# Splitting the weights of later phases during the Mamba phase, and storing the parts

## The chip, the cores and the metric

The kernel runs on one core of one Trainium2 chip. The metric is device time in microseconds (us) of one execution. A core has five instruction queues that run on their own: TensorE (PE, matmuls and transposes, results in PSUM), VectorE (DVE), ScalarE (ACT), GpSimd (POOL) and SyncE (SP, which here issues nearly all DMAs, that is, transfers between DRAM and the on-chip memory SBUF). Each queue is served strictly in order. An instruction that has to wait (for a semaphore that another engine or a landed DMA raises) holds up everything behind it on its own queue.

## What is computed

The reference is one layer of a hybrid encoder over 4096 tokens of width 1024. All three groups of heads read the same normalised input:

```python
h = rmsnorm(x, pre_norm_w)
u = h @ w_in                               # 1024 x 3208
y_ssm  = mamba2_group(u[:, :1544], ...)    # conv, chunked scan, gate, norm
y_rwkv = rwkv7_group(u[:, 1544:2696], ...) # r, k, v, g, decay latents; delta-rule state
y_mem  = memory_xattn_group(u[:, 2696:], mem_k, mem_v)
x + rmsnorm(concat(y_ssm, y_rwkv, y_mem) @ w_out, post_norm_w)
```

`mem_k` and `mem_v` are one projection, `rmsnorm(mem) @ w_mem_kv`, of 256 memory tokens. Everything is float32.

## The kernel before

**How a large product is done.** A float32 product is made from two rounded operands. Each matrix is split into a part in the type float32r, called hi, and the rounded remainder, called lo. The product is then three matmuls, hi*hi, hi*lo and lo*hi, for each of the 8 blocks of 128 rows. `proj_cm` (L145) and `proj_tm` (L155) issue them. For the input, `split_T` makes the two parts once for each stripe of 256 tokens, and `store_hT` writes them to DRAM (`hTd`), so that later phases read them back finished with `load_hT`.

**How the weights are split.** A raw weight block `w_st` is loaded by DMA (L70); ACT multiplies it with the norm's weight into hi (L80), and DVE forms lo in one instruction from the raw block, the same scale and hi (L81). For the output projection there is no scale (L85, L86). `split_w` and `load_w` do this at the place where a phase starts, so the weights of a phase are split at its seam with the phase before.

**The phases.** There are 16 stripes. `phase_a` (Mamba) loops over them: `stage1` of stripe i (z, x, B, C projections, convolution) is woven with `stage2` of stripe i-1 (the scan) and with `build_hT` of stripe i+1. `phase_b` (RWKV) starts with the last `stage2` as a tail beside its own first `stage1`, for which `load_b` loads and splits five matrices (the latents `lat`, then k, r, v, g). `stage1` first projects `lat`, then the first half of k, and then calls `lora`, whose matmuls (L642) need `wls`, made from the small tile `wl` (L556). Then it loops over the stripes. `phase_c` starts beside the tail of the RWKV recurrence: `memory` loads the memory tokens `mt` (L1076), normalises and transposes them (L132) and projects them with two split matrices; `qg` projects the queries with weights that `load_qg` split (L1015, L1016); `load_o` and `load_o2` split the two halves of the output weights `wo0` and `wo1`. Then it loops over the stripes.

**What sets the order.** `weave` takes the next piece of work from several generators in proportion to weights, and a scheduler places the instructions on each queue by a model of when each is ready. So a change in one place can move rows on every engine, but on the chip the rows of a queue are fixed. Buffers are tiles of pools with a fixed number of slots; a slot's next use waits for the last reader of its former one. `stage2` uses POOL for five large instructions for each chunk of 128 tokens, two chunks a stripe: `xde` (L427), `xst` (L428), `y` (L452), `prev` (L449) and a mask on `R` (L406). `R` is a row of decays, stored and read back by DMA (L382, L386). The convolution is 24 DVE instructions for each stripe (L338).

## Time and profile before

| | |
|---|---|
| time, median of 3 runs (lowest, highest) | 2209.92 us (2208.5, 2213.29) |
| the profiled execution's own time | 2211.41 us |
| its span, first to last instruction | 2209.6 us |
| busy: PE / DVE / ACT / POOL | 97% / 68% / 53% / 33% of the span |
| Mamba loop | to about 748 us, about 46 us for each stripe |
| seam of Mamba and RWKV | about 727 to 842 us |
| RWKV loop, seam to phase C | to about 1455 us, about 1455 to 1650 us |

A row of a timeline gives the start in us, the duration in us, the engine, the line and operation with output and inputs, how many equal rows were merged (x4), and in brackets the idle time of that engine before it and what ended it. A row of groups gives busy time in us and the mean of one in ns, and then idle time before it. A row of windows gives, for a stretch of time, the busy time of each engine and its number of instructions, then the granted TensorE clock as a share of full speed, the busy share of the DMA engines and GB/s. DMA-issuing rows of SP are marked SPq.

### The profile page before, as it was taken

Reading aid. Unit: us, or ns where it says so; the run is one execution under the profiler, and the core shown is the slowest. Engines: PE = TensorE matmul, PEld = TensorE weight load, DVE = VectorE, ACT = ScalarE, POOL = GpSimd, SP = SyncE. Lnnn points to the kernel's source line nnn. Section 1 sums busy time; section 2 is a strip of 40 time slices with the busy share of each in tenths; the row PEclk is TensorE's granted clock in tenths of the full one; section 3 lists DMA queues with packets and bytes.
Section 4 is the critical chain, followed back from the end, with each engine's and each line's share of the span. In section 5 each row is a group of like instructions: output and inputs, shape, how many; then the busy total and the mean of one; then the engine's idle time right before and its main releaser. Section 6 shows DMA issues by size and latency. Waiting matters only on the chain.

```text
span 2209.6 us, 50991 instructions
## 1 busy us (share of the span) xinstructions
PE 2151.8 (97%) x20705; PEld 1982.7 (90%) x20705; DVE 1502.7 (68%) x3405; ACT 1181.1 (53%) x2873; POOL 726.7 (33%) x1043
## 2 busy tenths in 40 slices
PE   8999999999999889999999999998999999999998
PEld 8999999999999788898898998987888888888986
DVE  7778788878888876577776777777573444444452
ACT  7555555555553565566666666677553333333441
POOL 2443443434433333334334333333112222222223
PEclk9999999999999999999999999999899999999999
DMA  6422233222332321111111121123243334333332
GB/s 212 148 97 87 97 134 106 97 87 96 131 109 106 118 87 40 45 64 63 50 45 45 45 83 49 45 89 129 83 172 134 125 110 162 110 133 132 100 123 77
DMA packets 82570, 218.86 MB, mean 99 GB/s; under 512 B 8151, under 2 KB 44446, under 8 KB 70046
## 3 DMA queue, kind: packets, MB, share of 16 engines
q1 hardware_dynamic: 81294, 215.59, 28.3%
q8 instruction: 163, 2.67, 0.5%
q14 instruction: 73, 0.60, 0.1%
q10 hardware_dynamic: 1040, 0.00, 0.0%
HBM read 152.00 MB, written 63.57 MB: 98 GB/s over the span
## 4 chain that ended last, share of the span: by engine, by line
PE 84%; DVE 7%; DMA 4%; ACT 3%; issue 1%; POOL 1%; SPq 0%; POOLq 0%; ACTq 0%; DVEq 0%
PE ps_pj L145 40%; PE ps_yd L155 8%; PE ps_pj L155 8%; PE ps_st L155 8%; DVE cc L338 2%; DMA R<-rowd 1%; PE ps_yd L467 1%; PE ps_yd L772 1%; PE ps_pj L1185 1%; PE ps_tr L132 1%; PE ps_yo L920 1%; PE ps_tr L1173 1%; PE ps_yo L927 1%; PE ps_st L459 1%; PE ps_yo L937 1%
## 5 line engine op out<-in xcount | busy, mean ns | idle before, releaser
L145 PE MATMUL ps_pj<-hh,w_hi 128*128 128x256 f32 x2704 | 790.5, 292 | 10.4 <-DVE cm L613 6.1
L145 PE MATMUL ps_pj<-hh,w_lo 128*128 128x256 f32 x2704 | 780.1, 289 | 0.2 <-DVE w_lo L81 0.2
L145 PE MATMUL ps_pj<-hl,w_hi 128*128 128x256 f32 x2704 | 777.2, 287 | 0.0
L145 PEld LDWEIGHTS ps_pj<-hh,w_hi 128*128 128x128 f32 x2704 | 520.2, 192 | 21.1 <-issue 6.3
L145 PEld LDWEIGHTS ps_pj<-hh,w_lo 128*128 128x128 f32 x2704 | 519.5, 192 | 6.8 <-DVE w_lo L81 0.7
L145 PEld LDWEIGHTS ps_pj<-hl,w_hi 128*128 128x128 f32 x2704 | 520.3, 192 | 5.9
L338 DVE SCALAR_TENSOR_TENSOR cc<-ux,cwh,cc 128x256 f32<-128x256 f32 x384 | 218.0, 610 | 15.4 <-ACT cc L335 15.1
L155 PE MATMUL ps_pj<-w_hi,hh 128*128 128x256 f32 (+1 forms) x528 | 155.6, 295 | 4.1 <-DVE zs L299 2.8
L155 PE MATMUL ps_pj<-w_lo,hh 128*128 128x256 f32 (+1 forms) x528 | 153.0, 290 | 0.0
L155 PE MATMUL ps_pj<-w_hi,hl 128*128 128x256 f32 (+1 forms) x528 | 152.2, 289 | 0.0
L1192 DVE TENSOR_TENSOR ya<-ps_pj,ya 64x256 f32<-64x256 f32 x64 | 26.9, 421 | 121.4 <-ACT ya L1191 121.0
L155 PEld LDWEIGHTS ps_pj<-w_hi,hh 128*128 128x128 f32 x528 | 102.1, 194 | 6.2 <-DVE zs L299 3.3
L1225 POOL TENSOR_TENSOR xr<-ot,xr 128x512 f32<-128x512 f32 x64 | 89.0, 1412 | 43.1 <-DVE ot L1224 43.1
L1219 POOL TENSOR_TENSOR sq<-sq 128x1 f32<-128x1 f32 x32 | 6.6, 207 | 292.9 <-ACT ot L1217 292.9
L155 PEld LDWEIGHTS ps_pj<-w_lo,hh 128*128 128x128 f32 x528 | 102.2, 194 | 0.3
L155 PEld LDWEIGHTS ps_pj<-w_hi,hl 128*128 128x128 f32 x528 | 102.0, 193 | 0.0
L155 PE MATMUL ps_st<-wo1l,yh 128*128 128x512 f32 x248 | 97.7, 394 | 1.0 <-DVE wo1l L1286 1.0
L155 PE MATMUL ps_yd<-wo0h,yh 128*128 128x512 f32 x248 | 98.2, 396 | 0.0
L155 PE MATMUL ps_st<-wo1h,yh 128*128 128x512 f32 x248 | 97.5, 393 | 0.0
L155 PE MATMUL ps_st<-wo1h,ylo 128*128 128x512 f32 x248 | 97.4, 393 | 0.0
L155 PE MATMUL ps_yd<-wo0h,ylo 128*128 128x512 f32 x248 | 97.3, 392 | 0.0
L155 PE MATMUL ps_yd<-wo0l,yh 128*128 128x512 f32 x248 | 97.2, 392 | 0.0
(468 smaller groups left out, 5106.8 us busy)
## 6 DMA issues: line engine op xcount, KB each, us to landing
hl<-hTd SPq DMA_DIRECT2D x32, 1024.0 KB, 5.1
hh<-hTd SPq DMA_DIRECT2D x32, 1024.0 KB, 8.3
xt<-in_x_dram SPq DMA_DIRECT2D x32, 512.0 KB, 3.5
...
```

The source lines that it names most:

```text
L132: te.transpose(pt[:, q * P:(q + 1) * P], src[:, k * P:(k + 1) * P], ident)
L145: te.matmul(outp, lhsT=a[:, k, :], rhs=b[:, k, :], start=(n == 0), stop=(n == 3 * KB - 1))
L155: te.matmul(outp, lhsT=a[:, k, tsl], rhs=b[:, k, 0:ncol], start=(n == 0), stop=(n == 3 * KB - 1))
L338: v.scalar_tensor_tensor(out=cc[:, b_, :], in0=ux[:, b_, j:j + NT], scalar=wj(j), in1=cc[:, b_, :], op0=ALU.mult, op1=ALU.add)
L459: te.matmul(pst[:, gr * 256:gr * 256 + 256], lhsT=q[c]["btm"][:, gr * P:(gr + 1) * P], rhs=q[c]["xde"][:, gr * 256:gr * 256 + 256], start= ...
L467: te.matmul(yd[hf * 64:hf * 64 + 64, h * 64:h * 64 + 64], lhsT=R[:, h, hf * 64:hf * 64 + 64], rhs=xdt[:, h * 64:h * 64 + 64], start=True, ...
L772: te.matmul(pa[:, c_ * P:(c_ + 1) * P], lhsT=BK[hs, p_, c_].rearrange("p a t -> p (a t)"), rhs=AR[hs, p_, c_].rearrange("p a t -> p (a t)" ...
L920: te.matmul(pch[hs, p_ * C:p_ * C + C], lhsT=AT[:, pc, h, 0:C], rhs=UV[:, pc, h, :], start=True, stop=True)
L927: te.matmul(pch[hs, 128 + p_ * C:128 + p_ * C + C], lhsT=TT[hs, pc].rearrange("p a t -> p (a t)"), rhs=X[hs, p_, :], start=True, stop=True)
L937: te.matmul(pch[hs, 256 + p_ * C:256 + p_ * C + C], lhsT=BKt[:, pc, hs], rhs=UV[:, pc, h, :], start=True, stop=True)
L1192: v.tensor_tensor(out=ya[hs], in0=pg[hs], in1=ya[hs], op=ALU.add)
L1225: g.tensor_tensor(out=xr[:, cs], in0=ots[n_], in1=xr[:, cs], op=ALU.add)
```

## The change

From the second stripe of the Mamba loop on, a new generator, `split_later`, splits the eleven matrices that RWKV, the memory, the queries and gates and the output projection need. It handles a job of 256 rows by up to 256 columns at a time: SP loads the raw block into `sp` (two slots), ACT writes hi into `sphi` (one slot), POOL multiplies the raw block by the scale in place (not for the output weights), POOL subtracts hi, and SP stores both parts in DRAM (`parts`). There are 52 jobs: 4 for `lat`, 4 for each of eight matrices with a scale, and 16 without a scale. The weave offers four jobs for each stripe. Where the later phases had loaded and split, `load_parts` now loads finished parts by four DMAs, twice the bytes of the raw matrix. DVE takes no part in these splits any more. In `phase_b` the order of loading is lat, v, g, k, r; the weight of its first `stage1` in the weave is 28 where it was 48; the staging pools of the seams are gone.

```diff
+    later = {"lat": (w2d, C_RW + 1024, P), "k": (w2d, C_RW + 256, 256), "r": (w2d, C_RW, 256), "v": (w2d, C_RW + 512, 256),
+             "g": (w2d, C_RW + 768, 256), "mk": (w_mem_kv, 0, 256), "mv": (w_mem_kv, 256, 256), "q": (w2d, C_XQ, 256),
+             "xg": (w2d, C_XG, 256), "o0": (wo2d, 0, 512), "o1": (wo2d, 512, 512)}
+    def split_later(pool):
...
+        def load(nm, c, kq):
...
+            st = pool.tile([P, 2, 256], F32R, name="sp", tag="sp", bufs=2)
+            sy.dma_start(out=st[:, :, 0:n].bitcast(F32),
...
+            hi = pool.tile([P, 2, 256], F32R, name="sphi", tag="sphi")[:, :, 0:n]
+            if nm[0] == "o":
+                s.copy(out=hi, in_=st)
+            else:
+                scale = (col("memw") if nm[0] == "m" else pnc)[:, kq * 2:kq * 2 + 2]
+                for k in range(2):
+                    s.activation(out=hi[:, k, :], in_=st[:, k, :], func=AF.Copy, scale=scale[:, k:k + 1])
+                g.tensor_tensor(out=st, in0=st, in1=scale.unsqueeze(2).broadcast_to([P, 2, n]), op=ALU.mult)
+            g.tensor_tensor(out=lo, in0=st, in1=hi.bitcast(F32), op=ALU.subtract)
+            yield
+            for n_, t_ in enumerate((hi, lo)):
+                sy.dma_start(out=parts[nm][:, n_, kq * 2:kq * 2 + 2, c:c + n], in_=t_.bitcast(F32))
+
+    def load_parts(nm, w):
+        for half in range(2):
+            ks = slice(half * 4, half * 4 + 4)
+            for n_ in range(2):
+                sy.dma_start(out=w[n_][:, ks, :].bitcast(F32), in_=parts[nm][:, n_, ks, :])
...
+            if i:
+                later_ = later_ or split_later(aw)
+                streams.append((some(4), 4))
...
-        def load_b():
-            for c_, w_ in ((1024, wlat), (256, wk), (0, wr), (512, wv), (768, wg)):
-                yield from load_w(w2d, C_RW + c_, w_, pnc, wsb)
+        for nm, w_ in (("lat", wlat), ("v", wv), ("g", wg), ("k", wk), ("r", wr)):
+            load_parts(nm, w_)
...
-        weave((a_tail, 10), (chain(load_b(), stage1(0, hT0, r0_)), 48))
+        weave((a_tail, 10), (stage1(0, hT0, r0_), 28))
...
+            load_parts("mk", wk_)
             mT = new_hT()
...
-            yield from load_w(w_mem_kv, 0, wk_, col("memw"), cm, 2)
...
-            yield from load_w(w_mem_kv, 256, wv_, col("memw"), cm, 2)
+            load_parts("mv", wv_)
...
+            load_o(wr, 0)
...
-        drain(load_o2(2))
+        load_o(cw, 1)
```

The first place is POOL in the second stripe's scan, its second chunk's rows from the mask to the `prev` of the next state. Before:

```order
L406 AFFINE_SELECT R<-R 128x1024
L427 TENSOR_TENSOR xde<-xdt,de 128x512
L428 TENSOR_TENSOR xst<-xst,bc_154 128x512
L452 TENSOR_TENSOR y<-y,xst 128x512
L124 TENSOR_SCALAR rs<-rs 128x1
L125 TENSOR_TENSOR rs<-rs,mhalf 128x1
L449 TENSOR_TENSOR prev<-prev,cd 128x512
```

The same stretch of POOL with the change (L194 is the multiplication and L195 the subtraction of a job; `sp` and `sphi` are the job's tiles):

```order
L440 AFFINE_SELECT R<-R 128x1024
L194 TENSOR_TENSOR sp<-sp,pnc 128x512
L195 TENSOR_TENSOR sp<-sp,sphi 128x512
L461 TENSOR_TENSOR xde<-xdt,de 128x512
L462 TENSOR_TENSOR xst<-xst,bc_165 128x512
L194 TENSOR_TENSOR sp<-sp,pnc 128x512
L486 TENSOR_TENSOR y<-y,xst 128x512
L195 TENSOR_TENSOR sp<-sp,sphi 128x512
L114 TENSOR_SCALAR rs<-rs 128x1
L483 TENSOR_TENSOR prev<-prev,cd 128x512
L115 TENSOR_TENSOR rs<-rs,mhalf 128x1
```

Two jobs now stand ahead of and between the rows of the scan. The scheduler did not keep to four jobs a stripe. There are two masks for each stripe on POOL; 5 subtractions stand ahead of the second mask, then 7, 8, 8, 8, 10 and 6 from one stripe's second mask to the next one's (the last 16 without a multiplication), and none after that.

The second place is SP at the seam of Mamba and RWKV, from the first `R` row of the last scan on (`ysT` are stores of Mamba's output). Before:

```order
L386 DMA R<-rowd_9881 128x1024
L70 DMA w_st<-in_w_in_dram 128x2x128 x4
L489 DMA ysT_107<-yT 512x1x128
L70 DMA w_st<-in_w_in_dram 128x2x256 x2
L386 DMA R<-rowd_9881 128x1024
L119 DMA hl<-hTd_78 128x2048
L119 DMA hh<-hTd_78 128x2048
L70 DMA w_st<-in_w_in_dram 128x2x256 x2
L489 DMA ysT_107<-yT 512x1x128
L556 DMA wl<-in_w_dram 64x256
L557 DMA wl<-in_a_dram 64x256
```

With the change, from the last two of the four loads of k on (ahead of them stand the first `R` row and the loads of lat, v and g, 4 rows each):

```order
L204 DMA w_hi<-parts_k 128x1024
L204 DMA w_lo<-parts_k 128x1024
L523 DMA ysT_107<-yT 512x1x128
L420 DMA R<-rowd_10328 128x1024
L204 DMA w_hi<-parts_r 128x1024
L204 DMA w_lo<-parts_r 128x1024
L204 DMA w_hi<-parts_r 128x1024
L204 DMA w_lo<-parts_r 128x1024
L109 DMA hh<-hTd_78 128x2048
L109 DMA hl<-hTd_78 128x2048
L596 DMA wl<-in_w_dram 64x256
L597 DMA wl<-in_a_dram 64x256
```

The small tile `wl` and the second `R` row now stand behind whole matrices. The loads of k wait for the slot of Mamba's x weights whose last matmul is 48 matmuls ahead of the loop's end, and those of r for the slot that is read by the last one.

The third place is PE at the seam to phase C, the rows up to the transposes of the memory tokens (L145 here are the query projections). Before:

```order
L920 MATMUL ps_yo<-UV,AT 64x64 x4
L145 MATMUL ps_pj<-hl,w_hi 128x256
L145 MATMUL ps_pj<-hh,w_lo 128x256
L145 MATMUL ps_pj<-hh,w_hi 128x256
L145 MATMUL ps_pj<-hl,w_hi 128x256
L145 MATMUL ps_pj<-hh,w_lo 128x256
L145 MATMUL ps_pj<-hh,w_hi 128x256
L145 MATMUL ps_pj<-hl,w_hi 128x256
L145 MATMUL ps_pj<-hh,w_lo 128x256
L145 MATMUL ps_pj<-hh,w_hi 128x256
L145 MATMUL ps_pj<-hl,w_hi 128x256
L132 MATMUL ps_tr<-ident,mt 128x128 x8
```

With the change (all of these are small matmuls of the recurrence's tail):

```order
L760 MATMUL ps_tr<-rkl,hones 128x256
L959 MATMUL ps_yo<-UV,AT 64x64 x4
L811 MATMUL ps_tr<-AR,BK 128x128 x4
L966 MATMUL ps_yo<-X,TT 64x64 x4
L122 MATMUL ps_tr<-ident,mt 128x128 x8
L996 MATMUL ps_yd<-UV,AT 64x64 x3
L976 MATMUL ps_yo<-UV,BKt 64x64 x4
L996 MATMUL ps_st<-UV,AT 64x64 x3
L122 MATMUL ps_tr<-ident,mt 128x128 x4
L993 MATMUL ps_yd<-ST,rr 64x64
L993 MATMUL ps_st<-ST,rr 64x64
L122 MATMUL ps_tr<-ident,mt 128x128 x4
```

The query projections, which stood ahead of these transposes, now stand behind all of them. On SP the load of `mt`, which was the first of its seam, stands behind the four loads of the memory's k weights.

More of the change, by code (lines that the diff above doesn't have):

```diff
@@ L516, in phase_a, with some @@
         hT = hT0
-        prev_r = None
+        prev_r, later_ = None, None
+        def some(n):
+            for _ in range(n):
+                if next(later_, later_) is later_:
+                    return
+                yield
         for i in range(NS):
@@ L540, in phase_b @@
         wcB = right("wcB", 1)
-        ws_s = ExitStack()
-        wsb = ws_s.enter_context(tc.tile_pool(name="wsb", bufs=2, side="right", reuse_waits="tile"))
         C = 64
@@ L1042, in phase_b @@
                          stack(r2), stage3(i, r2), stage4(i, r2))
[L1043 removed]
+            left_ = weave((gram, 10), (solve, 22), (back, 26), (first, 28), (load_qg(r2), 10), until=first)
         keep = dram.tile([P, 2, 2, NT], F32, name="keep")
@@ L1230, in phase_c, with load_o @@
         wo = []
-        def load_o(pool, st, n_):
-            if n_ % 2 == 0:
-                wo.append((pool.tile([P, KB, 512], F32R, name=f"wo{n_ // 2}h"), pool.tile([P, KB, 512], F32R, name=f"wo{n_ // 2}l")))
-            yield from load_w(wo2d, 256 * n_, half_of(n_), None, st, 1, (v,))
-        def half_of(n_):
-            return tuple(t_[:, :, (n_ % 2) * 256:(n_ % 2) * 256 + 256] for t_ in wo[n_ // 2])
+        def load_o(pool, n_):
+            wo.append((pool.tile([P, KB, 512], F32R, name=f"wo{n_}h"), pool.tile([P, KB, 512], F32R, name=f"wo{n_}l")))
+            load_parts(f"o{n_}", wo[n_])
         tail = b_tail(Ys[0])
-        late = ExitStack()
         hTc = []
@@ L1253, in start @@
             second_set()
-            both = [units(Ys[0], qsets[0], None), chain(*(load_o(wr, ws, n_) for n_ in range(2))), qg(hTc[0], qsets[1], 8)]
+            both = [units(Ys[0], qsets[0], None), qg(hTc[0], qsets[1], 8)]
             while both:
@@ L1274, in phase_c @@
         b_l.close()
-        late.close()
         cw = ctx.enter_context(tc.tile_pool(name="cw", bufs=1, reuse_waits="tile"))
-        def load_o2(n_):
-            if n_ == 2:
-                wo.append((cw.tile([P, KB, 512], F32R, name="wo1h"), cw.tile([P, KB, 512], F32R, name="wo1l")))
-            w_ = half_of(n_)
-            for half in range(2):
-                ks = slice(half * 4, half * 4 + 4)
-                st = cw.tile([P, D], F32, name="xr", tag="xr", bufs=2).rearrange("p (k c) -> p k c", c=256)
-                sy.dma_start(out=st, in_=wo2d[half * 4 * P:(half + 1) * 4 * P, 256 * n_:256 * n_ + 256].rearrange("(k p) c -> p k c", p=P))
-                s.copy(out=w_[0][:, ks, :], in_=st)
-                v.tensor_tensor(out=w_[1][:, ks, :], in0=st, in1=w_[0][:, ks, :].bitcast(F32), op=ALU.subtract)
-                yield
-        drain(load_o2(2))
+        load_o(cw, 1)
         pnw = cw.tile([P, D], F32, name="pnw")
```

59 lines of the change are left out of this document (24 added, 35 removed).

## The prediction

> **What bounds the kernel now.** I read the page first (span, busy time, slices, granted clock), then windows by stage, then the waits of PE, then timelines where they pointed.
>
> ```profile
> span 2209.6 us, 50991 instructions
> PE 2151.8 (97%) x20705; PEld 1982.7 (90%) x20705; DVE 1502.7 (68%) x3405; ACT 1181.1 (53%) x2873; POOL 726.7 (33%) x1043
> PE   8999999999999889999999999998999999999998
> PEclk9999999999999999999999999999899999999999
> ```
>
> PE is the bound: it is busy for all but 2209.6 - 2151.8 = 57.8 us. The same matmuls are issued after the change, so it can save only PE's idle time and the time at a lowered clock. The windows show where these are.
>
> ```profile
> 216.00:676.00 460.00, 457.50 (x4145) 444.91 (x4144) 375.25 (x759) 238.49 (x536) 181.92 (x258) 1.00 0.30 103
> 748.00:771.00 23.00, 14.41 (x112) 12.15 (x111) 21.80 (x50) 14.52 (x36) 8.85 (x10) 0.83 0.49 171
> 771.00:797.00 26.00, 19.89 (x151) 18.39 (x149) 22.41 (x42) 18.79 (x47) 13.86 (x15) 0.83 0.39 102
> 797.00:842.00 45.00, 42.24 (x468) 41.36 (x469) 34.55 (x94) 26.33 (x60) 15.67 (x22) 0.88 0.15 54
> 1510.00:1541.00 31.00, 29.93 (x285) 27.54 (x286) 24.66 (x71) 22.98 (x51) 6.06 (x11) 1.00 0.60 204
> 1541.00:1600.00 59.00, 53.50 (x637) 48.00 (x637) 33.21 (x76) 34.51 (x94) 7.15 (x15) 0.83 0.27 87
> ```
>
> The first row is ten stripes of Mamba, 46.0 us each: PE is full there, and DVE is at 375.25/460 = 82%. At the seam of Mamba and RWKV (748 to 842) PE idles 8.6 + 6.1 + 2.8 = 17.5 us, and the clock takes 23 x 0.17 + 26 x 0.17 + 45 x 0.12 = 13.7 us: 31 us that could be won. At the seam to phase C (1510 to 1600) it is 1.1 + 5.5 idle and 59 x 0.17 = 10.0 of clock: 17 us.
>
> **Part 1: the splits go from the seams (gain).** At the first seam these leave DVE and ACT (the row gives minimum, median and maximum in ns, and first and last start):
>
> ```profile
> L81 DVE SCALAR_TENSOR_TENSOR w_lo<-w_st,pnc,w_hi x40: 341/478/1267, 734.4 to 799.3; 128x256 fp32r<-128x256 f32 x32, 128x128 fp32r<-128x128 f32 x8
> L80 ACT ACTIVATE w_hi<-w_st,pnc x40: 385/495/510, 731.0 to 794.4; 128x256 fp32r<-128x256 f32 x32, 128x128 fp32r<-128x128 f32 x8
> PE ps_pj L145 <- DVE cm L613: 6.1, 1, 6.1
> PE ps_pj L145 <- ACT cc L335: 2.7, 1, 2.7
> PE ps_tr L416 <- ACT btm L423: 2.6, 1, 2.6
> ```
>
> DVE loses 40 instructions, about 19 us of the 44 it is busy from 748 to 797, and it is DVE's and ACT's queues that PE waits for (the last three rows). What is late next is a transfer. `lora` needs the small tile `wl`, which now stands behind the loads of r (2 MB) and of the next stripe's h (2 MB); the second `R` row stands behind k.
>
> ```profile
> 744.35 0.40 SPq L386 DMA_DIRECT2D R<-rowd  x1
> 754.30 0.63 SPq L556 DMA_DIRECT2D wl<-in_w_dram  x1
> 771.19 0.58 PE L642 MATMUL ps_pj<-lt,wls 128*128 128x256 f32 x1
> 747.93 0.28 PE L145 MATMUL ps_pj<-hh,w_lo 128*128 128x256 f32 x1
> 749.50:753.00 3.50, 2.12 (x18) 2.12 (x19) 2.74 (x8) 1.74 (x5) 1.03 (x3) 1.00 1.00 420
> ```
>
> The loads of r can start when Mamba's last matmul ends, at 748.2 (fourth row: start 747.93, 0.28 long). Full DMA engines move 420 GB/s (last row), so r, h and a 0.5 MB `R` take 4.7 MB/0.42 = 11 us, with some 2 us to start and land: `wl` arrives near 761, and after its casts `lora` can start near 764. PE itself would be there near 758 (48 matmuls, 0.12 us apart, and some small ones). So `lora`, now at 771.2, comes 7 us earlier, with some 2 us of the scan's matmuls moved ahead of it. Behind it the wait of 6.1 us goes, since no split is left in DVE's queue. Of the half-clock time behind 771 I credit 3 us, since a new gap of some 5 us before `lora` will bring some of its own. Sum: 7 + 2 + 6 + 3 = **18 us gained**. Bounds: 6 (`wl` as late as now) and 31 (all of the loss).
>
> **Part 2: the seam to phase C (nothing, -8 to +10).** The splits of queries, memory and output weights leave, worth at most the 17 us. But the load of `mt` now waits behind 2 MB of the memory's weights, and its transposes stand ahead of the query projections, which covered that time.
>
> ```profile
> 1509.81 0.81 SPq L1076 DMA_DIRECT2D mt<-in_mem_dram  x2
> 1521.17 1.04 PE L132 MATMUL ps_tr<-ident,mt 128*128 128x128 f32 x8
> ```
>
> Now `mt` is issued at 1509.8 and transposed 11.4 us later, with PE busy 29.9 of 31 us. Behind 2 MB (4.8 us at 420 GB/s) the transposes can't come earlier, and PE has only the recurrence's short matmuls until then: 5 to 8 us idle and some half clock. I set this against half of the 17 us, at zero. The output weights (4 MB, 10 us for each half) have time: `wo0` is loaded some 25 us ahead of its use.
>
> **Part 3: 52 jobs in the Mamba loop (loss).** PE is full there, so what delays its suppliers costs. POOL's and DVE's instructions with two SBUF inputs do not run at the same time:
>
> ```profile
> 306.81 2.53 DVE L338 SCALAR_TENSOR_TENSOR cc<-ux,cwh,cc 128x256 f32<-128x256 f32 x6 [0.41 <-ACT cc L335]
> 318.26 1.22 DVE L405 TENSOR_TENSOR R<-R,acs 128x1024 f32<-128x1024 f32 x1
> 319.40 4.08 DVE L338 SCALAR_TENSOR_TENSOR cc<-ux,cwh,cc 128x256 f32<-128x256 f32 x4
> 318.49 1.89 POOL L427 TENSOR_TENSOR xde<-xdt,de 128x512 f32<-128x512 f32 x1 [4.47 <-DVE xdt L425]
> 320.35 1.22 POOL L428 TENSOR_TENSOR xst<-xst,bc 128x512 f32<-128x512 f32 x1
> 300.33 1.04 POOL L428 TENSOR_TENSOR xst<-xst,bc 128x512 f32<-128x512 f32 x1
> 301.46 1.27 POOL L452 TENSOR_TENSOR y<-y,xst 128x512 f32<-128x512 f32 x1
> ```
>
> Six convolution steps alone take 0.42 us each; four beside POOL's rows take 1.02 each, and L427 takes 1.89 where 1.04 is its time. So a POOL instruction costs DVE some 0.6 to 0.8 us when it meets such a step. A job adds 1.04 (one operand broadcast, like L428) and 1.27 (two full operands, like L452), 2.31 us. At 8 jobs a stripe POOL gets 18.5 us more, and its present 182/10 = 18 makes 37 of 46 before any wait.
>
> Two ways to the price. By room: DVE's two-input work in a stripe is 24 x 0.42 = 10 for L338 and, from the rows below, (27.4 + 24.4 + 17.6 + 15.0 + 13.7)/10 = 10, and POOL's ten large rows take 11 us (6 x 1.04, 4 x 1.27, the mask taken like L452); with 18.5 that is 49.5 us, **3.5 over the 46** with no gap left. By DVE's queue: 16 instructions at 0.8 are 13 us, and its idle time is (460 - 375)/10 = 8.5, **4.5 over**; but half of that idle time is not free, since DVE stands waiting for POOL's short chain `sq` (41.5 us in the row, 4 a stripe), which now has jobs ahead of it, and for `R` by DMA, whose queue carries 6 MB more in 46 us (130 GB/s on top of 103).
>
> ```profile
> L342 DVE SCALAR_TENSOR_TENSOR cc<-th,cc 128x512 f32<-128x512 f32 x40 | 27.4, 684 | 0.1
> L405 DVE TENSOR_TENSOR R<-R,acs 128x1024 f32<-128x1024 f32 x20 | 24.4, 1221 | 0.0
> L479 DVE SCALAR_TENSOR_TENSOR y<-y,sq,nw 128x256 f32<-128x256 f32 x40 | 17.6, 482 | 41.5 <-POOL sq L476 41.5
> L470 DVE TENSOR_TENSOR y<-y,zs 128x512 f32<-128x512 f32 x20 | 15.0, 752 | 0.3
> L425 DVE TENSOR_TENSOR xdt<-xst,dt 128x512 f32<-128x512 f32 x20 | 13.7, 686 | 0.0
> L403 DVE TENSOR_TENSOR de<-R,acs 128x8 f32<-128x8 f32 x20 | 3.3, 164 | 9.5 <-DMA R<-rowd 9.5
> ```
>
> I take 7 us for a stripe with 8 jobs (bounds 1 and 11). The rows of POOL give 7 + 8 + 8 + 8 = 31 such jobs, 3.9 stripes: 27 us. Stripes with subtractions alone (10 x 1.27 = 12.7) just fit: 1 us. **28 us lost**, bounds 5 and 45. ACT's 16 added instructions of 0.5 us fit in its idle half.
>
> POOL's tiny rows (`rs`, `sq`, halo) are left out of the room, because the trace lets DVE's run beside them:
>
> ```profile
> 441.73 0.38 DVE L362 SCALAR_TENSOR_TENSOR p__6052<-p__6052,w__6051 128x16 f32<-128x16 f32 x2
> 442.13 0.17 DVE L363 SCALAR_TENSOR_TENSOR p__6052<-p__6052,w__6050 128x16 f32<-128x16 f32 x1
> 442.34 0.17 DVE L365 SCALAR_TENSOR_TENSOR dt<-p__6052,ab 128x16 f32<-128x16 f32 x1
> 441.94 0.57 POOL L125 TENSOR_TENSOR rs<-rs,mhalf 128x1 f32<-128x1 f32 x1
> ```
>
> L362 to L365 run at 0.17 us inside POOL's 0.57. The Trainium skill ("SBUF — State Buffer", section "Who interferes with whom") says of the port pair that DVE and GpSimd share that the first to issue holds it for its whole instruction and the other fully blocks. The large rows agree with that; these do not, so a short GpSimd instruction does not hold it for the time the profile gives it. By the rule's word the tiny rows would take 5 us of room more for each stripe, some 20 us more in all.
>
> **The sum.** 2211.4 (the profiled execution; 1.8 us lie outside its span, and it is 1.5 above the median of the runs) + 28 - 18 + 0 = **2221 us**.
>
> **Rivals.** (a) *POOL hides it*: the jobs fall where DVE reads PSUM or waits, so Mamba loses only the lower bound, 5, and the seams give 18 and 8: 2211 - 21 = **2190**. For it: PE's Mamba stripes have hardly an idle us now in spite of POOL. Against it: the room is 3.5 us short at perfect packing. (b) *They cancel*: 3 to 4 us a stripe, about 15, against 18: **2209**. (c) *In-order waits pile up* (slower still): ACT's next hi waits for the landing of the last one's store (one slot `sphi`), DVE for `R`, and PE's gaps bring half clock into Mamba; 5 us a stripe more, or the 20 us of the port rule: **2242**. The sign turns where the loop loses what the seams win: 18/31 = 0.6 us for each of the 31 jobs, or 26/31 = 0.8 with (a)'s 8 us at phase C.
>
> **How the numbers follow.** Forecast, 2212 to 2232: 0.45; (a), 2180 to 2205: 0.25; (b), 2206 to 2213: 0.13; (c), over 2232: 0.17. What this kernel's measurement can tell from no change is about 0.2%, 4.4 us, so faster means under 2205.5: 0.25; the same, up to 2214: 0.17; slower: 0.58. The range leaves out 0.1 on each side, the lower part of (a) and the end of (c): **2190 to 2245**.
>
> **What would show it.** Mamba stripes 2 to 6 at 50 to 54 us, L338 beside L194 and L195 at about 1 us, and PE idle there on `y`, `xde` or `cc`: Part 3. PE's wait before `lora` as the largest of the first seam, and the 6.1 us wait on `cm` gone: Part 1. PE idle before the transposes of `mt`: Part 2. Stripes at 46 to 47 us would prove Part 3 wrong, and with it the sign.

## The result, and the profile after

The change makes the kernel slower: median 2269.23 us (2265.57 to 2270.81, 4 runs) against 2209.21 us, a ratio of 1.0265 with an interval of 1.0251 to 1.028. The profiled execution has a span of 2268.9 us, 59.3 more than before. The page of the changed kernel, its head and two rows of its slices:

```profile
span 2268.9 us, 51349 instructions
PE 2178.1 (96%) x20705; PEld 2006.1 (88%) x20705; DVE 1506.3 (66%) x3321; ACT 1179.7 (52%) x2877; POOL 827.9 (36%) x1131
PE   8889989999999979999999999999999999999998
PEclk9999999999999999999999999998999999999999
```

PE issues the same 20705 matmuls, and is busy 26.3 us longer with them, which goes with a lower clock (0.977 in the mean, 0.986 before). The other 33 us are idle time. The first three slices, 170 us, show an 8 where before only the first did. To see which stage lost what, I follow four landmarks through both kernels: the last convolution step on ACT (the end of the Mamba loop, called *loop end* below), the product of the decay latents (`lora`), the transposes of the memory tokens, and the end. Timelines at the loop end, before and then after (the row merges two steps; the second starts at 750.3 and 801.1):

```profile
749.81 1.01 ACT L335 ACTIVATE cc<-ps_pj,cwh 128x256 f32<-128x256 f32 x2
```

```profile
800.59 1.02 ACT L369 ACTIVATE cc<-ps_pj,cwh 128x256 f32<-128x256 f32 x2
823.69 0.58 PE L682 MATMUL ps_pj<-lt,wls 128*128 128x256 f32 x1 [7.99 <-DVE lt L666]
1573.87 1.54 PE L122 MATMUL ps_tr<-ident,mt 128*128 128x128 f32 x6 [0.95 <-ACT mt L1109]
```

| stage, us | before | after | difference | forecast |
|---|---|---|---|---|
| start to loop end | 750.3 | 801.1 | +50.8 | +28 |
| loop end to `lora` | 20.9 | 22.6 | +1.7 | -18, with the 6 us behind `lora` |
| `lora` to the memory's transposes | 750.0 | 750.2 | +0.2 | |
| transposes to end | 688.4 | 695.1 | +6.7 | 0 |

**The loop.** Windows from 77 us to the loop end, before and after (length, PE busy, PEld, DVE, ACT, POOL, then the granted clock, the DMA share and GB/s):

```profile
77.00:750.00 673.00, 667.82 (x6055) 648.81 (x6054) 549.03 (x1108) 346.33 (x788) 262.61 (x370) 1.00 0.30 105
```

```profile
77.00:801.00 724.00, 684.83 (x6052) 661.78 (x6050) 580.42 (x1100) 372.71 (x851) 362.63 (x447) 0.98 0.45 153
```

PE's idle time is 724.0 - 684.8 = 39.2 us against 5.2, so 34 of the 51 us are waits. The other 17 are the same matmuls at a lower clock (0.98 in the row). Stripes with many jobs take 53 to 55 us each (GpSimd's second `xst` comes every 53.2 to 55.3 us); two windows of the changed kernel, one such stripe and the first stretch behind them:

```profile
207.00:262.00 55.00, 50.72 (x432) 48.77 (x431) 46.25 (x79) 30.91 (x71) 39.57 (x43) 0.94 0.61 204
371.00:419.00 48.00, 44.07 (x403) 42.62 (x403) 38.59 (x77) 23.99 (x54) 19.05 (x27) 1.00 0.30 100
```

PE's waits from 77 to 750 before, all of them, and the largest from 77 to 800 after (us in total, times, longest):

```profile
PE ps_tr L486 <- DVE y L479: 2.8, 4, 1.2
PE ps_yo L446 <- DVE prev L461: 0.4, 1, 0.4
```

```profile
PE ps_pj L145 <- ACT cc L369: 20.4, 5, 4.8
PE ps_tr L520 <- DVE y L513: 6.9, 6, 2.4
PE ps_g L405 <- DVE dta L401: 3.6, 3, 2.6
PE ps_yo L480 <- DVE prev L495: 2.1, 2, 1.6
```

The wait on `cc` comes five times, once in a stripe, and takes 3.3 to 4.8 us (it ends at 112.8, 167.8, 222.1, 276.2 and 333.5). Timelines around the third one, by engine:

```profile
208.22 2.69 DVE L372 SCALAR_TENSOR_TENSOR cc<-ux,cwh,cc 128x256 f32<-128x256 f32 x2
213.07 3.09 DVE L372 SCALAR_TENSOR_TENSOR cc<-ux,cwh,cc 128x256 f32<-128x256 f32 x3
216.25 0.63 ACT L375 ACTIVATE th<-cc 128x512 f32<-128x512 f32 x1 [2.81 <-DVE cc L372]
217.74 0.91 ACT L193 ACTIVATE sphi<-sp,pcol 128x256 fp32r<-128x256 f32 x2 [0.86 <-POOL sp L195]
218.56 1.04 ACT L113 ACTIVATE junk<-xt 128x1024 bf16<-128x1024 f32 x1
221.02 1.02 ACT L369 ACTIVATE cc<-ps_pj,cwh 128x256 f32<-128x256 f32 x2
215.91 0.28 PE L145 MATMUL ps_pj<-w_hi,hl 128*128 128x256 f32 x1
216.03 0.28 PE L145 MATMUL ps_pj<-w_hi,hh 128*128 128x256 f32 x1
222.09 0.59 PE L145 MATMUL ps_pj<-w_hi,hh 128*128 128x264 f32 x1 [3.56 <-ACT cc L369]
222.48 0.42 PE L145 MATMUL ps_pj<-w_lo,hh 128*128 128x264 f32 x1
222.70 0.42 PE L145 MATMUL ps_pj<-w_hi,hl 128*128 128x264 f32 x1
```

Read from the bottom up. PE waits 3.56 us for a PSUM buffer that ACT's `cc` (L369) empties. ACT is late twice over: it had waited 2.81 us for DVE's convolution, whose steps take 1.03 to 1.35 us here beside GpSimd in place of 0.42, and 0.86 us for GpSimd's subtraction, which has to read `sphi` before the next hi may overwrite it. Behind the gap the matmuls start 0.22 us apart, where it was 0.12: the clock is halved, so the stall costs a second time. All five of these waits are followed by such a stretch (the granted clock is 0.66 to 0.79 in windows of 8 to 11 us around them), and so is one of 2.6 us at 80.7 (0.66 from 80 to 85).

**The first seam.** SP's queue, ACT's casts of the small tile `wl` with the row that ACT waited for ahead of them, a window, and two of DVE's rows further on, in the changed kernel:

```profile
798.45 0.32 SPq L204 DMA_DIRECT2D w_hi<-parts_r  x1
804.78 0.32 SPq L109 DMA_DIRECT2D hl<-hTd  x1
805.49 0.56 SPq L596 DMA_DIRECT2D wl<-in_w_dram  x1
818.07 0.42 ACT L507 ACTIVATE xst<-y 128x256 f32<-128x256 f32 x1 [2.73 <-DVE y L504]
818.88 1.64 ACT L602 CAST wls<-wl 64x256 fp32r<-64x256 f32 x4
820.87 0.86 DVE L604 TENSOR_TENSOR wll<-wl,wls 64x256 fp32r<-64x256 f32 x2
785.00:815.00 30.00, 26.44 (x244) 24.22 (x243) 24.61 (x49) 9.97 (x22) 12.88 (x13) 1.00 1.02 395
878.40 1.20 DVE L845 TENSOR_TENSOR t<-N,T 128x36 f32<-128x36 f32 x1
880.04 0.15 DVE L653 TENSOR_TENSOR cm<-ps_pj,pcol 128x2 f32<-128x2 f32 x1
```

The DMA engines are full for 30 us, from 785 to 815, and `wl` is issued at 805.5, near the end of that. PE's wait of 8.0 us ahead of `lora` (the L682 row above) is for `lt`, which DVE forms at 823.2 behind `wll` at 820.9, behind ACT's casts. The casts start at 818.9 right behind `xst` of the last scan, for which ACT had waited 2.73 us; no row waits for the landing of `wl` itself, whose packets end at 817.0 in the trace. So two things come late there at nearly the same time, the tile and the scan's rows in front of its casts.

Behind `lora`, a wait on `cm` is still there: `cm` (L653) stands in DVE's queue behind the steps of the solve (L845), and PE waits 4.3 us for it, until 880.3. In the kernel before, what stood in front of `cm` were splits, one of which had waited for ACT's hi:

```profile
792.54 0.96 DVE L81 SCALAR_TENSOR_TENSOR w_lo<-w_st,pnc,w_hi 128x256 fp32r<-128x256 f32 x1 [1.36 <-ACT w_hi L80]
796.48 0.15 DVE L613 TENSOR_TENSOR cm<-ps_pj,pcol 128x2 f32<-128x2 f32 x1
```

They are gone, but the solve has come in their place, and 1.8 of the 6.1 us are won.

**The second seam.** PE's clock there, and the whole stage from the transposes to the end, in the changed kernel and then in the one before:

```profile
1566.00:1586.00 20.00, 17.78 (x117) 15.19 (x117) 13.26 (x40) 13.43 (x26) 6.34 (x10) 0.50 0.35 120
1573.80:2268.90 695.10, 676.78 (x4424) 599.83 (x4424) 325.56 (x681) 262.64 (x710) 146.41 (x241) 0.98 0.37 130
```

```profile
1521.10:2209.60 688.50, 670.69 (x4399) 594.45 (x4398) 339.64 (x708) 274.99 (x736) 145.23 (x241) 0.98 0.36 123
```

PE waits only 0.95 us ahead of the first transpose of `mt` (the L122 row above). In the stage it is idle 18.3 us, and 17.8 before, so waits do not make the difference. It is busy 6.1 us longer, and its clock is at half from 1566 to 1586, around the transposes, although no wait of PE in the ten us ahead of that is longer than 1.03 us.

### The profile page after: what moved, and what is told of

It reads as the page before. It is cut to its first block, busy times and chain, and to the rows that moved or that the text cites. A ratio compares the mean times of both kernels' runs of the same rounds, so it can differ in the third digit from the quotient of the medians.

```text
span 2268.9 us, 51349 instructions
## 1 busy us (share of the span) xinstructions
PE 2178.1 (96%) x20705; PEld 2006.1 (88%) x20705; DVE 1506.3 (66%) x3321; ACT 1179.7 (52%) x2877; POOL 827.9 (36%) x1131
## 4 chain that ended last, share of the span: by engine, by line
PE 78%; DVE 8%; DMA 5%; ACT 3%; POOL 3%; issue 2%; SPq 0%; POOLq 0%; ACTq 0%; DVEq 0%
PE ps_pj L135 35%; PE ps_yd L145 8%; PE ps_st L145 7%; PE ps_pj L145 7%; DVE cc L372 3%; DMA xt<-in_x_dram 1%; DMA R<-rowd 1%; PE ps_pj L1213 1%; PE ps_tr L1201 1%; PE ps_yo L959 1%; PE ps_st L811 1%; PE ps_yo L966 1%; PE ps_yd L811 1%; PE ps_yo L976 1%; PE ps_tr L122 1%
## 5 line engine op out<-in xcount | busy, mean ns | idle before, releaser
L372 DVE SCALAR_TENSOR_TENSOR cc<-ux,cwh,cc 128x256 f32<-128x256 f32 x384 | 232.1, 646 | 41.2 <-ACT cc L369 40.9
L145 PE MATMUL ps_pj<-w_hi,hh 128*128 128x256 f32 (+1 forms) x528 | 160.6, 306 | 23.1 <-ACT cc L369 20.4
L145 PE MATMUL ps_pj<-w_lo,hh 128*128 128x256 f32 (+1 forms) x528 | 157.7, 299 | 0.0
L145 PE MATMUL ps_pj<-w_hi,hl 128*128 128x256 f32 (+1 forms) x528 | 157.3, 299 | 0.0
L145 PEld LDWEIGHTS ps_pj<-w_hi,hh 128*128 128x128 f32 x528 | 107.0, 203 | 26.7 <-ACT cc L369 22.4
L145 PEld LDWEIGHTS ps_pj<-w_lo,hh 128*128 128x128 f32 x528 | 107.1, 203 | 0.2
L145 PEld LDWEIGHTS ps_pj<-w_hi,hl 128*128 128x128 f32 x528 | 106.9, 203 | 0.0
L145 PE MATMUL ps_yd<-wo0h,yh 128*128 128x512 f32 x248 | 99.8, 402 | 2.8 <-DVE ot L1252 2.8
L145 PE MATMUL ps_yd<-wo0l,yh 128*128 128x512 f32 x248 | 98.3, 396 | 0.0
L145 PE MATMUL ps_yd<-wo0h,ylo 128*128 128x512 f32 x248 | 98.2, 396 | 0.0
L145 PE MATMUL ps_st<-wo1l,yh 128*128 128x512 f32 x248 | 97.7, 394 | 0.0
L145 PE MATMUL ps_st<-wo1h,yh 128*128 128x512 f32 x248 | 97.7, 394 | 0.0
L145 PE MATMUL ps_st<-wo1h,ylo 128*128 128x512 f32 x248 | 97.4, 393 | 0.0
```

The source lines that it names most:

```text
L145: te.matmul(outp, lhsT=a[:, k, tsl], rhs=b[:, k, 0:ncol], start=(n == 0), stop=(n == 3 * KB - 1))
L372: v.scalar_tensor_tensor(out=cc[:, b_, :], in0=ux[:, b_, j:j + NT], scalar=wj(j), in1=cc[:, b_, :], op0=ALU.mult, op1=ALU.add)
```

## The experiments

All ratios but the change's own are to runs of the kernel before on the same chip, where its median was 2201.7 to 2204.7 us. That is 0.2 to 0.3% under the 2209.2 beside the change, so 750.3 there stands for some 748.5 here, and 801.1 for some 799: what is won against 801.1 below may be 2 us too large. A loop end is read from one profile.

| run | loop end, us | ratio (interval) |
|---|---|---|
| no_jobs / no_jobs_order | 745.0 / 749.1 | 1.0048 (1.0031 to 1.0064) / 0.9961 (0.9946 to 0.9976) |
| the change | 801.1 | 1.0265 (1.0251 to 1.028) |
| no_pool | 768.2 | 1.0134 (1.0119 to 1.015) |
| tiny_pool | 790.6 | 1.0228 (1.0212 to 1.0244) |
| lo_on_dve | 789.9 | 1.0231 (1.0213 to 1.0248) |
| store_1_row | 789.5 | 1.0255 (1.024 to 1.0271) |
| dma_only | 785.3 | 1.0201 (1.0182 to 1.0219) |
| four_a_stripe | 808.9 | 1.0287 (1.0267 to 1.0307) |
| four_no_pool | 773.4 | 1.0153 (1.0117 to 1.0188) |
| four_tiny | 799.1 | 1.029 (1.0261 to 1.0318) |
| four_dve | 781.3 | 1.0202 (1.0177 to 1.0228) |
| four_own | 805.2 | 1.0261 (1.0245 to 1.0276) |
| four_act | 789.7 | 1.0193 (1.0172 to 1.0213) |
| four_tiny_act | 770.3 | 1.0093 (1.0067 to 1.0119) |
| four_no_pool_act | 760.7 | 1.0057 (1.0042 to 1.0072) |
| four_dve_order | 777.0 | 1.0109 (1.0087 to 1.0131) |
| all_act | 764.7 | 1.0014 (1.0002 to 1.0026) |
| few | 747.9 | 0.9983 (0.997 to 0.9995) |

The first two rows differ in two loads, no work, and their loops by 4 us: placing alone moves the loop by that much, and smaller differences are not read below.

**1. Is it GpSimd's data, the waits, or the bytes?** Four runs in the dense stripes of the change.

```diff
 no_pool
-                g.tensor_tensor(out=st, in0=st, in1=scale.unsqueeze(2).broadcast_to([P, 2, n]), op=ALU.mult)
-            g.tensor_tensor(out=lo, in0=st, in1=hi.bitcast(F32), op=ALU.subtract)
 store_1_row
-                sy.dma_start(out=parts[nm][:, n_, ...], in_=t_.bitcast(F32))
+                sy.dma_start(out=parts[nm][0:1, n_, ...], in_=t_[0:1].bitcast(F32))
 lo_on_dve
-            g.tensor_tensor(out=lo, in0=st, in1=hi.bitcast(F32), op=ALU.subtract)
+                    v.scalar_tensor_tensor(out=lo[:, k, :], in0=st[:, k, :], scalar=scale[:, k:k + 1],
+                                           in1=hi[:, k, :].bitcast(F32), op0=ALU.mult, op1=ALU.subtract)
 dma_only
-            hi = pool.tile([P, 2, 256], F32R, name="sphi", tag="sphi")[:, :, 0:n]
-                    s.activation(out=hi[:, k, :], in_=st[:, k, :], func=AF.Copy, scale=scale[:, k:k + 1])
```

> Leaves out the two GpSimd instructions of each job (multiplication and subtraction), so lo is stored as the raw block and the output is not the layer's. Everything else of the change stays: loads, ACT's hi, stores, four loads of parts for each matrix. The last convolution step on ACT in the Mamba loop starts at 750.3 us before and at 801.1 with the change: 50.8 us lost there. Theory PORT (GpSimd's two-input instructions hold up DVE's two-input ones, and PE waits in the end): the loop is back at 750 to 756. Theory WAITS (one hi slot: ACT's next hi waits for GpSimd's subtraction and for the store, SP's stores wait behind it too, and R and x behind them): a part of that wait goes with the subtraction, the wait for the store stays: 765 to 785. Theory BYTES (39 MB more through the DMA queues delay R and x): hardly a change, 790 to 801.

> The stores of the jobs write 1 of 128 partitions, with the same instructions and waits, so 26 MB less is stored in the Mamba loop; the later loads read finished parts of the input instead, the same number of bytes, so the output is not the layer's. Last convolution step on ACT: 750.3 before, 801.1 with the change. BYTES: back to 755 to 770. PORT: 798 to 802. WAITS: 785 to 800 (a smaller store lands a little earlier).

> lo is formed on DVE in two instructions from raw block, scale and hi, as the kernel before did at its seams; GpSimd has no part in the jobs. DVE gets 8 x 2 x 0.42 = 6.7 us more for a stripe of 8 jobs, and is idle 8.5 of 46 there. PORT: the loop is back at 750 to 760. WAITS: ACT's next hi now waits for DVE's queue in place of GpSimd's, so most of the loss stays, 780 to 801. BYTES: 790 to 801.

> The jobs only load and store: no hi on ACT, nothing on GpSimd; the raw block is stored twice, so the output is not the layer's. 768.2 without GpSimd's instructions, 18 us over before. ACT (hi waits in ACT's in-order queue for the raw block's landing, and the convolution's copies behind it): back to 750 to 757. BYTES (R and x land later): 763 to 769; the store of one row took 11.5 us off, which speaks for a part of it, some 759 to 763.

PORT fails in all of the first three, BYTES in the first two, and it misses the third by 0.1 us. Without GpSimd 33 of the 51 us go (768.2), smaller stores win 11.6 us (789.5), DVE in GpSimd's place 11 (789.9). All three lie within the ranges of WAITS, but these are 15 to 21 us wide, and by them alone it is not shown which of its waits counts. The last run is the surprise: loads and stores alone (785.3) cost 17 us more than loads, hi and stores (768.2). So the parts do not add up. Without hi nothing paces the jobs: their last raw block is loaded at 254.9 us (284.3 in no_pool, 360.2 in the change). DVE and ACT wait 51 us for `R` in this loop, where it is 28 in no_pool, and ACT 52 us for x, where it is 38. That the closer transfers make R and x late fits this; no run changes it alone.

**2. Does the crowding cost?** The job's hi is tied to a point of its stripe, so that four jobs fall in each stripe.

```diff
-            for _ in range(n):
-                if next(later_, later_) is later_:
+            for n_ in range(n):
+                while len(r.get("pts", ())) <= n_:
+                    yield
+                with tc.issue_after(r["pts"][n_]):
+                    if next(later_, later_) is later_:
```

> The jobs are unchanged, but ACT's hi of each is tied to a point of its stripe (the tanh of the z-projections and the copies of the x-projections, two of each), so that four jobs fall in each of 13 stripes in place of 5 to 10 in seven. PORT, by room: 49.5 - 4 x 2.31 = 40.3 us of port work in 46, so next to nothing is lost: 750 to 757. WAITS and BYTES with the same cost for each job: 52 jobs as before, 50.8 us, 790 to 801; with a cost that grows with the crowding, in between.

> Four jobs a stripe, and the two GpSimd instructions of each job left out (lo is stored raw; the output is not the layer's). At four a stripe the second chunk's R is subtracted 29.6 us after acT where it is 27.6 before, and the first one 5.6 where 5.3, so SP's queue is nearly free of the jobs; the last convolution step on ACT starts at 808.9, 58.6 us over before. GPSIMD (at four a stripe the whole loss is GpSimd's two instructions): 750 to 757. SP AND BYTES (loads and stores cost the same for each job wherever it stands, 18 us for 52 as without GpSimd in the dense stripes): 766 to 772.

> Four jobs a stripe with lo on DVE in two instructions of about 0.42 us each, 3.4 us more for a stripe, of 8.5 us in which DVE is idle. ROOM (work that fits in the idle time is hidden): 750 to 757. CHAIN (PE waits for the end of a chain through DVE in each stripe, so what DVE gets more delays it, hidden or not): up to 3.4 x 13 = 44 us, 785 to 795; in between, the part of DVE's idle time that stands ahead of PE's waits.

The room theory falls at once: 808.9 us, worse than the dense stripes, though port work would fill 40 of 46 us by the prediction's count. A job costs (808.9 - 748.5)/52 = 1.2 us of the loop with four in every stripe. Without GpSimd it is 0.5 (773.4), with lo on DVE 0.6 (781.3, just under what CHAIN expected). Idle time of an engine did not hide them.

**3. Which of GpSimd's costs?** In its queue, instructions of 2 columns that take no less time (a power of 2 columns takes some 0.7 us; in four_tiny_act they are busy 2.6 us for each job, the real ones 2.1 in four_act).

```diff
-            g.tensor_tensor(out=lo, in0=st, in1=hi.bitcast(F32), op=ALU.subtract)
+            g.tensor_tensor(out=lo[:, 0, 0:2], in0=st[:, 0, 0:2], in1=hi[:, 0, 0:2].bitcast(F32), op=ALU.subtract)
+            g.tensor_scalar(out=tp, in0=st[:, 0, 0:2], scalar1=0.0, scalar2=1.0, op0=ALU.mult, op1=ALU.add)
+            for _ in range(1 if nm[0] == "o" else 3):
+                g.tensor_tensor(out=tp, in0=tp, in1=mhalf[:, 0:2], op=ALU.pow)
```

> Each job's multiplication and subtraction on GpSimd are replaced by a subtraction and a scaling of 2 columns and three powers of 2 columns (one for the output weights), in a chain behind ACT's hi: about 0.2 + 0.2 + 3 x 0.6 = 2.2 us of GpSimd's queue for a job, nearly as now, with next to no data. lo is stored raw, so the output is not the layer's. The last convolution step on ACT starts at 750.3 before, 801.1 with the change, 768.2 without the two instructions. PORT (it is the data of GpSimd's two-input instructions that holds up DVE): 767 to 774. QUEUE (it is the 2.3 us that each job stands ahead of the scan's rows in GpSimd's in-order queue, and ACT's and SP's waits for its end): 790 to 802.

> Four jobs a stripe, with GpSimd's two instructions replaced by the chain of instructions of 2 columns, nearly as long on its queue (lo is raw; the output is not the layer's). Here SP's queue is out of the way, so it tells the two ways in which GpSimd can cost time apart. PORT (GpSimd's data holds up DVE): within 5 us of the run without GpSimd's instructions. QUEUE (the scan's rows stand behind the job in GpSimd's queue): within 10 us of the 808.9 with them.

Both gave the same split, at 790.6 and 799.1: 22 to 26 us come back with instructions that move nothing, and the data adds 10. That looked like QUEUE, but in these runs the stores on SP also wait for GpSimd, which the next runs take away.

**4. SP's queue.** Waits of SP from 77 to 750 us in four_no_pool (L196 are the stores of the jobs):

```profile
SPq L196 <- ACT sphi L193: 121.8, 24, 11.6
SPq L196 <- ACT sphi L189: 56.5, 8, 10.8
SPq L196 <- ACT ea L410: 55.4, 13, 5.0
SPq L196 <- DMA sp<-in_w_in_dram: 52.5, 25, 4.5
```

By these four rows SP stands 286 of 673 us in front of stores of the jobs, and the loads of R and x stand behind them. That alone proves little, since in the kernel before SP stands 220 us in front of the stores of Mamba's output. So the stores go to other queues:

```diff
-            yield
-            for n_, t_ in enumerate((hi, lo)):
-                sy.dma_start(out=parts[nm][:, n_, ...], in_=t_.bitcast(F32))
+            for n_, t_ in enumerate((hi, lo)):          # four_no_pool_act, four_tiny_act
+                s.dma_start(out=parts[nm][:, n_, ...], in_=t_.bitcast(F32))
+            for n_, t_, e_ in ((0, hi, s), (1, lo, g)):  # four_own
+                e_.dma_start(out=parts[nm][:, n_, ...], in_=t_.bitcast(F32))
+            s.dma_start(out=o_, in_=i_)                  # four_act: lo, at the next job's point
```

> Four jobs a stripe without GpSimd's instructions (lo is stored raw; the output is not the layer's), and both stores are issued by ACT right behind its hi, so nothing of the jobs waits on SP but the load for its slot. Last convolution step on ACT: 750.3 before, 773.4 with the stores on SP. SP (stores that wait on SP hold up R, rowd and x): 750 to 757. ACT AND BYTES (hi takes 0.9 us of ACT's queue, and the bytes slow R): 768 to 778, or later for the time that ACT takes to issue.

> Four whole jobs a stripe, hi stored by ACT right behind forming it and lo by GpSimd right behind its subtraction; everything is computed. Last convolution step on ACT: 808.9 with the stores on SP. SP: its part of some 20 us goes, 785 to 792. GPSIMD'S AND ACT'S QUEUES: 800 to 815.

> Four jobs a stripe, both parts stored by ACT right behind hi (lo raw; the output is not the layer's), and on GpSimd for each job the chain of instructions of 2 columns, which nothing waits for but the slot's next use. Last convolution step on ACT: 760.7 with no GpSimd instruction in the jobs, 805.2 with the two real ones. PORT: 760 to 767. QUEUE: 795 to 806. If both have a part, as with the stores on SP (26 for the queue, 10 for the data): 780 to 790.

> Four whole jobs a stripe (GpSimd's two instructions as in the change), hi stored by ACT right behind forming it, lo by ACT at the next job's point. Everything is computed. Last convolution step on ACT: 760.7 with no GpSimd instruction, 770.3 with dataless ones of the same length, 805.2 with the real ones and GpSimd issuing lo's store. DATA (what GpSimd's instructions move is what costs): 795 to 803, since 41 us of issuing on GpSimd's queue at the rate of the dataless ones (9.7 us for some 114 us) is worth 3.5. ISSUE (GpSimd's stores were the cost in that run, and the data costs 10 as with the stores on SP): 778 to 784.

Without GpSimd the loop end goes from 773.4 to 760.7: the stores on SP were half of what was left. The way to PE is seen from 77 to 745 us, in four_no_pool and then in four_no_pool_act:

```profile
PE ps_pj L145 <- ACT cc L370: 15.0, 11, 3.3
ACT junk L113 <- DMA xt<-in_x_dram: 73.7, 24, 4.1
```

```profile
ACT junk L113 <- DMA xt<-in_x_dram: 52.7, 25, 3.6
```

ACT reads the next stripe's x (`xt`) ahead of `cc` in its queue. When x lands late, `cc` is late and PE waits, 15.0 us in all; with the stores on ACT that wait of PE is gone. The waits for R did not fall (41 us, then 48). Now a ladder can be read, at four jobs a stripe: 748.5 with no jobs; loads, hi and stores on ACT 760.7 (+12); GpSimd's queue without data 770.3 (+10); its data 789.7 (+19); the stores on SP again 808.9 (+19). Four_tiny_act lies in none of its three ranges, 3 us above PORT's, and four_act between its two: data counts for more than the queue, and GpSimd's issuing of the stores, 15.5 us (805.2), for more than I gave it. A rival for the 19 us would be that ACT waits for lo before it stores it, but in four_act every subtraction ends 0.39 us or more ahead of its store, and ACT is idle right ahead of the 52 stores for 6 us in all. What the data does is seen in DVE's convolution steps from 100 to 720 us, in four_tiny_act and then in four_act:

```profile
L378 DVE SCALAR_TENSOR_TENSOR cc<-ux,cwh,cc 128x256 f32<-128x256 f32 x312 | 173.6, 599 | 16.4 <-ACT cc L375 16.4
```

```profile
L379 DVE SCALAR_TENSOR_TENSOR cc<-ux,cwh,cc 128x256 f32<-128x256 f32 x300 | 192.2, 684 | 8.9 <-ACT cc L376 8.6
```

The mean step takes 0.68 us in place of 0.60, and there are 24 in a stripe. PE's largest wait in four_act and in four_tiny_act, from 60 to 800 us:

```profile
PE ps_tr L527 <- DVE y L520: 30.7, 14, 3.0
```

```profile
PE ps_tr L526 <- DVE y L519: 15.4, 13, 2.4
```

It is one place in each stripe: the transposes of the scan's output have their fixed place in PE's queue, `y` comes late at the end of a chain through DVE and GpSimd, and PE has nothing else it may do.

**5. The seams alone, and their order.** No jobs; then the small tile loaded early and the memory tokens ahead of their weights.

```diff
 no_jobs
-                streams.append((some(4), 4))
-                sy.dma_start(out=w[n_][:, ks, :].bitcast(F32), in_=parts[nm][:, n_, ks, :])
+                    sy.dma_start(out=w[n_][:, ks, c:e].bitcast(F32), in_=hTd[c // 256][:, n_, ks, 0:e - c])
 no_jobs_order, besides
+            if i == NS - 1:
+                wl = aw.tile([P, 256], F32, name="wl")
+                sy.dma_start(out=wl[0:64, :], in_=w2[0])
+                sy.dma_start(out=wl[64:128, :], in_=a2[0])
-            load_parts("mk", wk_)
+            mts = [cm.tile([P, D], F32, name="mt", tag="mt", bufs=2) for t in range(2)]
+            for t in range(2):
+                sy.dma_start(out=mts[t], in_=mem[0][t * P:(t + 1) * P, :])
+            load_parts("mk", wk_)
```

> No jobs at all in the Mamba loop; the later loads read finished parts of the input, the same bytes, so the output is not the layer's. The seams are those of the change. Last convolution step at 750 to 752. If the seams cost what the profile of the change shows (1.7 more to the decay latents' product, 6.7 more from the memory tokens' transposes to the end), the span is 2209.6 + 9 = 2217 to 2220: the change would lose with free splits too. If the seams lose only because the Mamba loop's late stores and loads run into them, they win what was forecast, 18 us: 2190 to 2196.

> As without jobs, and the small tile of the decay latents is loaded early in the Mamba loop into memory that is free without the jobs, and the memory tokens are loaded ahead of their weights. If PE's 8 us wait ahead of the latents' product is for that tile, the product comes 6 to 8 us earlier after the last convolution step (22.6 us with the change, 20.9 before): 15 to 17. If the wait is for the latents' weights or the projection of k, no more than 2 us are won. For the memory tokens: 4 to 7 us from their transposes to the end, if their late load is the cause; 0 to 2 if it is the clock alone.

> As four a stripe with lo on DVE, and the small tile of the latents is loaded early, into a raw block's slot that is free in the last stripe, and the memory tokens ahead of their weights. Everything is computed. Without any jobs these two orders took 7 us before the latents' product, 5 us in the RWKV loop and 8 us from the memory tokens on, off the seams of the change, and the span was 14.8 us under before. If the loop loses 5, the span is 2200, faster than before by 10; if it loses 15, they are equal; if 40, it is 2235.

With free splits the change still loses, by 0.48%: `lora` comes 22.7 us after the loop end, and the last stage takes 691.5. So the loop's late stores are not why the seam wins nothing. The order is. PE's largest waits around the first seam in no_jobs, and then in no_jobs_order:

```profile
PE ps_pj L681 <- DVE lt L665: 8.0, 1, 8.0
PE ps_pj L135 <- DVE cm L652: 4.6, 2, 4.3
```

```profile
PE ps_pj L135 <- DVE cm L653: 4.9, 1, 4.9
PE ps_pj L682 <- DVE lt L666: 0.6, 1, 0.6
```

With `wl` early, `lora` comes 13.7 us after the loop end, 9.0 sooner. That is not the transfer alone: the scheduler now also puts ACT's casts ahead of the scan's rows, 5.3 us behind the loop end where it was 17.9. With `mt` first the last stage takes 686.9, 4.6 less than in no_jobs, and 4.0 of these are PE's busy time. A wait on `cm` stays in both, without any split. With four jobs a stripe on DVE the same two orders take 2247.5 to 2226.6 us (4 of it in the loop), but the loop loses 28.

**6. Can a version win?** All 52 jobs on DVE and ACT with both orders, and the kernel before with only the 20 jobs of the RWKV matrices, two a stripe.

```diff
+            s.dma_start(out=parts[nm][:, 0, ...], in_=hi.bitcast(F32))
+            lo_st.append((parts[nm][:, 1, ...], lo.bitcast(F32)))
...
+            if lo_st:
+                o_, i_ = lo_st.pop()
+                s.dma_start(out=o_, in_=i_)
```

> Four jobs a stripe with lo on DVE, hi stored by ACT right behind forming it and lo by ACT at the next job's point, the latents' small tile early, the memory tokens ahead of their weights. Everything is computed. The loop's last convolution step: 777.0 with the stores on SP; the stores' part was 12.7 without GpSimd (773.4 to 760.7). IF THAT PART ADDS: 764, and a span of 2208, no difference from before that shows. IF DVE'S WORK TAKES THE SAME TIME ANYWAY: 773 to 778, 2217 to 2222.

> The kernel before with only the 20 jobs of the RWKV matrices, two a stripe, lo on DVE, stores on ACT, the latents' small tile early; the memory, the queries and the output weights are split at the second seam as before. Everything is computed. The 52 jobs cost 15 us in this form by the reading above, so 20 cost 4 to 6: the loop ends at 753 to 757; from there the latents' product 13.7 later, RWKV 745, and phase C 688 as before: 2200 to 2204, against 2209.6 before, faster by 0.2 to 0.4%. If a job costs 0.6 us as with the stores on SP, they cancel: 2208 to 2212.

The loop of all_act ends at 764.7, as the sum gave it, and it is 0.14% over before (0.02 to 0.26%). `few` ends its loop at 747.9, where 753 to 757 was expected, `lora` follows 13.7 us later, and it is 0.17% under before (0.05 to 0.3%), 2200.4 us against 2203.7. Both intervals are just clear of zero, and both differences lie within the 0.2% that the prediction takes for no change. So no version here that computes everything is clearly faster than before.

## Why the prediction was wrong

**What bounds the kernel** was right: PE, with stripes of 46.0 us that have no idle time. What followed from it was not drawn far enough. A queue that is always full has no way to catch up, so a wait of PE stays in the time, and a long one can bring the clock down as well: to 0.98 over the loop of the change, while four_no_pool, with waits of up to 3.3 us, keeps 1.00.

**Part 3, the loop (28 us, bounds 5 to 45; measured 50.8).** The sign and the main cause stood; three steps failed.
- *Room*. "By room" and "Stripes with subtractions alone ... just fit" took port work as a sum that fits into 46 us. The price of the crowded stripes was near, 7 us where they take 7 to 9 over 46. But the last of them, with subtractions alone, takes 53.2 us too, where such stripes were to cost 1 us in all; from the second `xst` at 98.2 to the one at 370.8 five stripes lose 43 of the 51 us. And at four a stripe the work fits by that count, and the loss was 60 us, not none. What counts is the chain to `cc` (20.4 us of PE's waits in the change) and `y` (6.9), whose readers have fixed places in PE's queue; `xde`, which the prediction also named, is 0.2. The price of 0.6 to 0.8 us for a GpSimd instruction that meets a DVE step fits the timeline above, where a step takes 0.6 to 0.9 us more; that DVE's idle time takes it up was wrong.
- *What was left at nothing*. "ACT's 16 added instructions of 0.5 us fit in its idle half", and SP was priced nowhere: neither that its stores wait for GpSimd, nor that x stands behind them. Loads, hi and stores cost 12 us with the stores on ACT and 25 with them on SP; no run has the price of hi alone. Rival (c) named in-order waits, but on ACT's hi and for another 15 to 20 us.
- *The clock*. The lower clock stood in (c) only; in the loop it is 17 of the 51 us.

The Trainium skill ("SBUF — State Buffer", section "Who interferes with whom") calls the shared port pair an exclusive lock, and says, of a DVE instruction in a mode with two ports, that who issues first gets it for the whole instruction. Read as the prediction read it, for every instruction with two inputs in SBUF, instructions of 2 columns and no less time should cost what the real ones do, 789.7 at four a stripe. They cost 770.3, and the real ones 19 us more: as the prediction had it from the tiny rows, a short one does not hold the pair for its time.

On the clock, the Trainium skill ("TensorE: Matmul & The Clock Gate", Part 1) has half rate after an idle window of about 3.4 us. The gap of 3.56 us above agrees. Shorter ones are not safe here: in the seam before, the gap of 2.7 us that ends at 750.9 leaves the clock at 1.00, but those of 2.6 and 2.3 us that end at 756.8 and 770.6 are followed by 0.50. And at the second seam of the change it falls to 0.50 with no gap over 1.03 us.

**Part 1, the first seam (18 us gained; measured 1.7 lost).** The step that failed is "r, h and a 0.5 MB `R` take 4.7 MB/0.42 = 11 us". It counted what is issued from the loop's end on, as if the DMA engines were idle then. They had been full since 785, with lat, v, g and k: 30 us at 395 GB/s are 12 MB. Nor did `lora` follow 3 us behind the tile: its casts stand behind the scan's rows, and it starts 6.7 us after the last packets of `wl`. The sign of it was named right, the wait ahead of `lora` as the largest of the seam. That the wait on `cm` would go with the splits was wrong: 4.3 to 4.9 of the 6.1 us stayed in every kernel without them. The relief of DVE was also read too large: of the 44 us that it is busy from 748 to 797, 28 of the 40 splits take 15, not 19, and the others lie outside that window.

**Part 2, the second seam (0, -8 to +10; measured 6.7 lost)** is within its bounds, but not by the way it was reckoned. PE idle for 5 to 8 us ahead of the transposes of `mt` was the sign to look for, and it waited 0.95 us. The loss is PE's lower clock, which the prediction had as "some half clock" without a price. That the late load of `mt` has a part in it fits no_jobs_order, where 4.6 us come back; how it brings the clock down is not shown.

**The sum.** 28 - 18 + 0 was 50.8 + 1.9 + 6.7, so 2221 us became 2269, above the stated 2190 to 2245; only the direction came out as forecast. Rival (c), at 2242, was nearest, and no rival had the splits losing on both sides. That GpSimd hides it, or that the two cancel, is refuted by the loop's windows.

**What stays open.** The ladder's rungs are one profile each, and the scheduler moves other rows with each edit, by up to 4 us where that could be seen. The rung of GpSimd's queue rests on a chain that is somewhat longer than the real work. At the dense placement of the change the parts do not add (785.3 against 768.2), so its 50.8 us are not divided exactly; only GpSimd's 33 and the rest's 18 are read there directly.
